# Attention in units of four heads and 128 queries instead of two heads, with 512-column value products and the compressed block filled to 128 keys

## The chip, the cores and the metric

The kernel runs on one core of one Trainium2 chip. The metric is the device time of one execution in microseconds (us). The kernel before takes 2535.07 us, the median of 3 runs (2532.68 to 2537.05).

## The reference, cut to what matters

The program is one transformer block over 1024 tokens with a width of 1024: a norm, one wide input projection, three mixers (sparse attention, RWKV-7, gated delta), gates and an output projection, then a squared-ReLU feed-forward. Only the sparse attention is touched. It has 8 heads of 64 in 2 key groups, so four heads share their keys and values. For each block of 128 queries it takes three softmaxes over the same queries: over 63 compressed keys, over the selected keys (with 16 selected blocks of 64 and 1024 tokens all causal keys are selected) and over a window of 512 keys. The three results are gated and added:

```python
s = jnp.einsum('bghqd,bgcd->bghqc', qq, kc) * scale
p_c = _masked_softmax(s, cmp_end[None, :] <= t[:, None])
o_c = jnp.einsum('bghqc,bgcd->bghqd', p_c, vc)
...
o_s = jnp.einsum('bghqk,bgqkd->bghqd', p_s, vsel)
...
o_w = jnp.einsum('bghqk,bgkd->bghqd', p_w, vwb)
o = gg[..., 0:1] * o_c + gg[..., 1:2] * o_s + gg[..., 2:3] * o_w
```

## The kernel before, in words

All products run in a split form: an operand is cast to the type fp32r (the high part) and the remainder is kept as a second tile (the low part), and products of the parts are summed in PSUM.

**Stages.** `build` (L1538) runs the norm and small columns, RWKV, the gated delta, then `nsa` (L1141), then the rest of the tail. `nsa` first prepares keys and values (`_nsa_kv`, `_nsa_compress`) and then runs `_nsa_attn` (L1267). The attention has two halves of 512 queries. `tail(0)` (L1412), the merge, output projection and feed-forward of the first 512 tokens, is put in hand as a second stream of work when the first half of the attention is written (`end_mixed`), and `tail(1)` follows when everything else is done.

**Units.** `_nsa_attn` makes 32 units. Unit u is one pair of heads `hp` by one block `qb` of 128 queries: half u // 16, pair u // 4 % 4, block u % 4 in its half. A `query` task per four units loads 512 queries of a pair, normalises them and splits them into `QH` and `QL`. `_nsa_head` (L1313) makes one head: for each of the three key sets the scores (L1339 to L1343, two products and the mask products, in one of 3 PSUM tiles "s"), the row maximum on VectorE (L1344), the exponential on ScalarE into a tile `P` (L1349), and at last the scaling of `P` by gate over sum (L1363; VectorE for the selected keys, GpSimd for the compressed and window keys). There are 4 tiles `P`, so two units have tiles at a time. `_nsa_pv` (L1366) multiplies with the values: for two blocks of 128 keys at a time, two heads each, four transposes into one PSUM tile "pt" (two of them), the cast to `PH` on ScalarE (L1391), the remainder `PL` on VectorE (L1392), then per block two products of 256 columns (`_pv_mm`, L1405) with the stationary tile V2s, V2w or V2c. The last block is the compressed one: it has 64 keys, so V2c is a stationary tile of 64 rows. `po` is then folded to `oT` (L1399 to L1402) and stored to `o_a` in HBM.

**Order of the work.** The kernel writes its instructions through a small planner, `run` (L167). A task gives back a wait in planned microseconds, or a condition, at each `yield`; the planner keeps a planned TensorE clock `te.time`. It steps the due task of lowest number. Beside it, it writes steps of the dense stream (three products of 512 columns, planned at 0.64): one for each 0.64 that attention steps have taken (`NBESIDE`, share 1.0), and one whenever no task is due. In the first half the dense stream is the remaining gate columns of the input projection (`fill`, tiles `fps<-hTh` and `fps<-hTl`), in the second it is `tail(0)`. Dense instructions get a priority number that is larger by 1000 (delta), and the first product of each step is tied behind the attention product written before it. Tile's scheduler then fixes each engine's order. Unit u may start when unit u-1 has written its heads and u-2 its value products; its value products wait for those of u-1. So the heads of one unit are planned beside the value products of the unit before.

```python
NBESIDE = (1.0, 1000, 0)
NLAT = (1.5, 3.0, 6.0, 0.3, 1.0, 3.0, 6.0, 0.6, 2.0, 0.8)
```

A head gives back 0.6 (`NLAT[7]`) after each of its three key sets, a unit 2.0 (`NLAT[8]`) between its heads and its value products, and the value products 0.8 (`NLAT[9]`) after each PSUM tile of transposes.

Of the kernel before, what the change touches and what calls it, by code (L numbers as in the profile page):

```python
# [19 lines left out]
P = 128  # L20
# [91 lines left out]
class Block:  # L112
# [1028 lines left out]
    def nsa(self):  # L1141
        tc = self.tc
        self.run(lambda: len(self.waiting) < 3 * KT and self.current is None)
        K2s, K2w = (self.tl(n, 1, [P, 2, S], F32R) for n in ("K2s", "K2w"))
        V2s, V2w = (self.tl(n, 1, [P, NST, 2, P], F32R) for n in ("V2s", "V2w"))
        K2c = self.tl("K2c", 1, [P, 2, 64], F32R)
        V2c = self.tl("V2c", 1, [64, 2, P], F32R)
        self.nsa_consts()
        self.share, self.delta, self.keep = NBESIDE
        outer = self.wk  # L1150
        with tc.tile_pool(name="nsap", bufs=1, reuse_waits="tile") as wk:
            self.wk = wk
            prep = [self.task(self._nsa_kv(br, half, K2, V2), br * 2 + half)
                    for br, (K2, V2) in enumerate(((K2s, V2s), (K2w, V2w))) for half in range(2)]
            prep.append(self.task(self._nsa_compress(K2c, V2c), 4))
            self.finish(*prep)
        with tc.tile_pool(name="nsaw", bufs=1, reuse_waits="tile") as wk:
            self.wk = wk
            self._nsa_attn(K2s, K2w, V2s, V2w, K2c, V2c)
        self.wk = outer  # L1160


    def norm64(self, x, gain, tag, out=None):
        nc = self.nc
        sq = self.tl(tag + "sq", 1)
        nc.scalar.activation(out=sq, in_=x, func=AF.Square)
        ps = self.mps("pt", 2)
        for i in range(4):
            self.te.matmul(ps[:, 2 * i:2 * i + 2], lhsT=sq[:, i * P:(i + 1) * P], rhs=self.blk64, start=True, stop=True)
        r = self.tl("r64", 2, [P, 8])  # L1170
        nc.scalar.activation(out=r, in_=ps[:, 0:8], func=AF.Sqrt, bias=self.eps)
        nc.vector.reciprocal(r, r)
        rb = self.tl(tag + "rb", 1)
        nc.gpsimd.tensor_copy(rb.rearrange("p (x d) -> p x d", d=64), r[:, :, None].to_broadcast([P, 8, 64]))
        yield NLAT[0]
        ps = self.mps("pt", 2)
# [26 lines left out]
    def _nsa_compress(self, K2c, V2c):  # L1203
        nc, a = self.nc, self.a
        tt, ts = nc.vector.tensor_tensor, nc.vector.tensor_scalar
# [3 lines left out]
        ps = self.mps("pt", 2)  # L1209
# [4 lines left out]
        ts(out=V2c, in0=self.ident[:64, None, :].to_broadcast([64, 2, P]), scalar1=0.0, scalar2=None, op0=OP.mult)  # L1214
        for x in range(2):
            kT = self.tl("kT", 1, [P, 2, S])
            src = self.nsa_in[4 + x].rearrange("(g d) s -> d g s", g=2)
# [10 lines left out]
            hp = self.mps("o", 1)  # L1228
# [9 lines left out]
            ps = self.mps("pt", 2)  # L1238
# [5 lines left out]
            ps = self.mps("pt", 2)  # L1244
# [21 lines left out]

    def _nsa_attn(self, K2s, K2w, V2s, V2w, K2c, V2c):  # L1267

        self.mark = mark = [0] * 32 + [9, 9]
        qs = {}  # L1270

        def query(i):
            half, hp = i // 4, i % 4
            nc = self.nc
            q = self.tl("q", 1)
            nc.sync.dma_start(out=q, in_=self.nsa_in[hp, :, half * 512:half * 512 + 512])
            yield NLAT[5]
            QH = self.tl("QH", 2, [P, 2, 512], F32R)
            QL = self.tl("QL", 2, [P, 2, 512], F32R)
            q = yield from self.norm64(q, self.qg, "q")  # L1280
            for e in range(2):
                h = slice(e * 64, e * 64 + 64)
                for x in (e, 1 - e):
                    nc.scalar.copy(QH[x * 64:x * 64 + 64, e], q[h])
                    nc.gpsimd.tensor_tensor(out=QL[x * 64:x * 64 + 64, e], in0=q[h], in1=QH[h, e].bitcast(F32), op=OP.subtract)
# [12 lines left out]
        self.finish(*units)  # L1298

    def _nsa_unit(self, u, qs, K, V):  # L1300
        half, hp, qb = u // 16, u // 4 % 4, u // 16 * 4 + u % 4
        g = hp // 2
        QH, QL = qs[u // 4]
# [6 lines left out]
        yield from self._nsa_pv(qb, g, hp, Ps, *V)  # L1310
        self.mark[u] = 2

    def _nsa_head(self, qb, g, H, QH, QL, K2s, K2w, K2c):  # L1313
        nc = self.nc
        tt, ts = nc.vector.tensor_tensor, nc.vector.tensor_scalar
        qs = slice(qb % 4 * P, qb % 4 * P + P)
# [18 lines left out]
        for b, pieces in enumerate(segs):  # L1335
            tiles = []
            for i, (c, keys, n, masks) in enumerate(pieces):
                ps = self.mps("s", 3)
                self.te.matmul(ps[:, :n], lhsT=QH[:, qs], rhs=keys, start=True, stop=False)  # L1339
                self.te.matmul(ps[:, :n], lhsT=QL[:, qs], rhs=keys, start=False, stop=not masks)  # L1340
# [25 lines left out]
    def _nsa_pv(self, qb, g, hp, Ps, V2s, V2w, V2c):  # L1366
        nc = self.nc
        tt = nc.vector.tensor_tensor
        k0 = max(0, qb - 4)
        blocks = [(kb * P, P, V2s[:, kb, g, :]) for kb in range(qb + 1)]  # L1370
        blocks += [(1024 + (kb - k0) * P, P, V2w[:, kb, g, :]) for kb in range(k0, qb + 1)]
        blocks += [(1664, 64, V2c[:, g, :])]
        po = self.mps("o", 1)[:, 0:256]
        last = len(blocks) - 1
        todo = []
        for b0 in range(0, len(blocks), 2):
            bl = blocks[b0:b0 + 2]
            ps = self.mps("pt", 2)
            for j, (c, n, v) in enumerate(bl):
                for e in range(2):  # L1380
                    self.te.transpose(ps[:n, (j * 2 + e) * P:(j * 2 + e + 1) * P], Ps[e][:, c:c + n], self.ident)
            PH = self.tl("PH", 3, [P, 512], F32R)
            PL = self.tl("PL", 3, [P, 512], F32R)
            runs = []
            for j, (c, n, v) in enumerate(bl):
                if runs and runs[-1][2] == n:
                    runs[-1][1] = (j + 1) * 256
                else:
                    runs.append([j * 256, (j + 1) * 256, n])
            for x0, x1, n in runs:  # L1390
                nc.scalar.copy(PH[:n, x0:x1], ps[:n, x0:x1])  # L1391
                tt(out=PL[:n, x0:x1], in0=ps[:n, x0:x1], in1=PH[:n, x0:x1].bitcast(F32), op=OP.subtract)  # L1392
            todo.append((b0, bl, PH, PL))
            if len(todo) == 2:
                self._pv_mm(po, *todo.pop(0), last)
            yield NLAT[9]
        self._pv_mm(po, *todo.pop(0), last)
        tmp = self.tl("otmp", 1, [64, 256])
        nc.scalar.copy(tmp, po[64:128])  # L1399
        oT = self.tl("oT", 2, [P, P])  # L1400
        for e in range(2):
            tt(out=oT[e * 64:e * 64 + 64], in0=po[0:64, e * P:(e + 1) * P], in1=tmp[:, e * P:(e + 1) * P], op=OP.add)  # L1402
        nc.sync.dma_start(out=self.o_spill["a"][hp, :, qb * P:(qb + 1) * P], in_=oT)

    def _pv_mm(self, po, b0, blocks, PH, PL, last):  # L1405
        for j, (c, n, v) in enumerate(blocks):
            x = slice(j * 256, (j + 1) * 256)
            self.te.matmul(po, lhsT=v, rhs=PH[:n, x], start=(b0 + j == 0), stop=False)
            self.te.matmul(po, lhsT=v, rhs=PL[:n, x], start=False, stop=(b0 + j == last))


    def tail(self, hf, wbufs):  # L1412
# [202 lines left out]
```

## Time and profile before

| | |
|---|---|
| median of 3 runs | 2535.07 us |
| profiled execution, its own time | 2527.64 us |
| its span | 2525.9 us |
| TensorE products busy | 2377.5 us (94%) |
| TensorE weight loads busy | 1907.6 us (76%) |
| VectorE / ScalarE / GpSimd busy | 1472.0 / 1043.1 / 986.8 us |
| mean granted TensorE clock | 0.965 |
| attention, first scores to last value product | 1170 to 1741 us of the span |

Engines are PE (TensorE product), PEld (its weight load), DVE (VectorE), ACT (ScalarE), POOL (GpSimd) and SP (SyncE). The duration of a product in the trace contains its way through the array, and products overlap: what one costs TensorE in a full stream is the distance from its start to the next start. A line of a timeline gives start, duration, engine, line, operation, tile written and tiles read, the rows and columns of the stationary tile (128\*128, 64\*128), the shape, and xN for N merged instructions.

### The profile page before, as it was taken

What the parts mean: (1) busy time and instruction counts of PE and PEld (TensorE: products, weight loads), DVE (VectorE), ACT (ScalarE), POOL (GpSimd) and SP (SyncE); (2) the same over time, 40 slices, a digit from 0 to 9 for tenths busy, and PEclk for the clock granted to TensorE, in tenths of its full rate; (3) what the DMA queues carried; (4) which work ended last, traced back from release to release, by engine and by line L of the source; (5) the groups of instructions that cost most, each with busy time, mean ns of one, the idle gap of its engine ahead of it and who ended that gap; (6) DMA issues with size and microseconds to landing.
All of it is one profiled execution on the core that took longest, in us unless ns stands there. A gap on an engine that the chain in (4) does not pass through costs nothing.

```text
span 2525.9 us, 37184 instructions
## 1 busy us (share of the span) xinstructions
PE 2377.5 (94%) x13589; PEld 1907.6 (76%) x13589; DVE 1472.0 (58%) x3197; ACT 1043.1 (41%) x2083; POOL 986.8 (39%) x975
## 2 busy tenths in 40 slices
PE   6979899999988999989999999999999998999999
PEld 4757676777776777777887777778888876788887
DVE  4586877663477567232556777766454436545444
ACT  5333433332344433225657665654332334423232
POOL 4444444333322121224545675344333346233232
PEclk9889889999999999989999999999999999999999
DMA  4222222222223122272213331014232354223232
GB/s 137 68 56 65 58 63 58 71 54 74 72 66 83 43 57 73 83 173 80 64 52 114 111 106 57 21 62 128 92 109 84 117 164 157 75 88 111 83 111 92
DMA packets 319718, 216.79 MB, mean 86 GB/s; under 512 B 78486, under 2 KB 273184, under 8 KB 319536
## 3 DMA queue, kind: packets, MB, share of 16 engines
q1 hardware_dynamic: 308672, 195.63, 27.3%
q10 hardware_dynamic: 9792, 17.83, 2.0%
q8 instruction: 107, 1.75, 0.3%
q0 software_dynamic: 1072, 0.96, 0.2%
q14 instruction: 75, 0.61, 0.1%
HBM read 178.16 MB, written 36.22 MB: 85 GB/s over the span
## 4 chain that ended last, share of the span: by engine, by line
PE 72%; DVE 13%; DMA 6%; ACT 4%; issue 2%; POOL 2%; SPq 0%; ACTq 0%; POOLq 0%; DVEq 0%
PE fps L97 53%; PE mps L97 15%; PE mps L101 3%; DVE inv_p L336 2%; DVE inv_u L338 1%; DVE gacc L882 1%; DVE BK L550 1%; DMA cw<-in_nsa_cmp_w_dram 1%; POOL wlo L259 1%; DMA lb<-inv 1%; ACT P L1349 1%; ACT whi L254 1%; DMA wraw<-in_w_branch_dram 1%; DVE ast L1344 1%; DMA gin<-gates 1%
## 5 line engine op out<-in xcount | busy, mean ns | idle before, releaser
L259 POOL TENSOR_TENSOR wlo<-wraw,whi 128x512 fp32r<-128x512 f32 (+2 forms) x408 | 530.0, 1302 | 878.9 <-ACT whi L254 848.5
L254 ACT CAST whi<-wraw 128x512 fp32r<-128x512 f32 (+1 forms) x408 | 286.6, 705 | 632.1 <-PE fps L97 444.8
L97 PE MATMUL fps<-hTh,whi 128*128 128x512 f32 x1024 | 447.3, 439 | 6.5 <-ACT rraw L424 3.5
L97 PE MATMUL fps<-hTh,wlo 128*128 128x512 f32 x1024 | 415.8, 410 | 1.3 <-POOL wlo L259 1.3
L97 PE MATMUL fps<-hTl,whi 128*128 128x512 f32 x1024 | 416.5, 408 | 0.0
L259 DVE TENSOR_TENSOR wlo<-wraw,whi 128x256 fp32r<-128x256 f32 (+1 forms) x207 | 129.7, 629 | 232.5 <-ACT whi L254 227.0
L97 PEld LDWEIGHTS fps<-hTh,whi 128*128 128x128 f32 x1024 | 200.9, 197 | 48.5 <-ACT rraw L424 3.6
L97 PEld LDWEIGHTS fps<-hTh,wlo 128*128 128x128 f32 x1024 | 200.0, 196 | 47.7 <-POOL wlo L259 2.2
L97 PEld LDWEIGHTS fps<-hTl,whi 128*128 128x128 f32 x1024 | 201.8, 197 | 32.3
L97 PE MATMUL fps<-h2h,whi 128*128 128x512 f32 x512 | 200.0, 391 | 1.3 <-DVE h2l L291 1.3
L1363 POOL TENSOR_SCALAR P<-P,ast 128x64 f32<-128x64 f32 (+5 forms) x128 | 137.2, 1088 | 160.0 <-DVE ast L1356 97.1
L97 PE MATMUL fps<-h2l,whi 128*128 128x512 f32 x512 | 199.6, 390 | 0.0
L97 PE MATMUL fps<-h2h,wlo 128*128 128x512 f32 x512 | 199.4, 390 | 0.0
L97 PE MATMUL fps<-whi,fl 128*128 128x512 f32 x512 | 191.0, 389 | 0.0
L97 PE MATMUL fps<-whi,fh 128*128 128x512 f32 x512 | 189.9, 391 | 0.0
L97 PE MATMUL fps<-wlo,fh 128*128 128x512 f32 x512 | 189.0, 389 | 0.0
L1442 DVE TENSOR_TENSOR acc<-fps,acc 128x512 f32<-128x512 f32 x160 | 106.7, 686 | 101.4 <-PE fps L97 101.0
L1349 ACT ACTIVATE P<-mps,ast 128x128 f32<-128x128 f32 (+4 forms) x256 | 124.9, 494 | 75.3 <-DVE ast L1347 45.5
L1344 DVE TENSOR_REDUCE ast<-mps 128x1 f32<-128x128 f32 (+4 forms) x256 | 109.0, 441 | 56.3 <-PE mps L97 53.5
L1392 DVE TENSOR_TENSOR PL<-mps,PH 128x512 fp32r<-128x512 f32 (+2 forms) x168 | 103.3, 619 | 47.7 <-ACT PH L1391 47.0
L1391 ACT CAST PH<-mps 128x512 fp32r<-128x512 f32 (+2 forms) x168 | 88.1, 533 | 63.5 <-PE mps L101 58.1
L97 PEld LDWEIGHTS fps<-h2h,whi 128*128 128x128 f32 x512 | 96.2, 188 | 21.5 <-DVE h2l L291 1.8
(465 smaller groups left out, 4802.0 us busy)
## 6 DMA issues: line engine op xcount, KB each, us to landing
wraw<-in_w_in_dram SPq DMA_DIRECT2D x152, 256.0 KB, 2.9
wraw<-in_w_ff_dram SPq DMA_DIRECT2D x128, 256.0 KB, 2.8
wraw<-in_w_ff_dram SPq DMA_DIRECT2D x64, 512.0 KB, 3.4
gates<-fst ACTq DMA_DIRECT2D x48, 256.0 KB, 2.0
wraw<-in_w_branch_dram SPq DMA_DIRECT2D x48, 256.0 KB, 3.2
gin<-gates SPq DMA_DIRECT2D x48, 256.0 KB, 3.2
wraw<-in_w_out_dram SPq DMA_DIRECT2D x16, 512.0 KB, 3.5
nsa_in<-fst ACTq DMA_DIRECT2D x20, 256.0 KB, 2.1
```

The costliest lines, as they stand in the source:

```text
L97: return self.note(self.nc.tensor.matmul(out, lhsT=lhsT, rhs=rhs, **kw))
L101: return self.note(self.nc.tensor.transpose(out, x, ident))
L254: nc.scalar.copy(hi, raw)
L259: eng.tensor_tensor(out=lo[:, x], in0=raw[:, x], in1=hi[:, x].bitcast(F32), op=OP.subtract)
L336: nc.vector.tensor_tensor(out=v, in0=lt[:n, s, None, s + 1:].to_broadcast([n, w, w]), in1=u[:n, s + 1:, s + 1:].rearrange("p t c -> p c t" ...
L338: nc.vector.tensor_reduce(out=u[:n, s, s + 1:], in_=v, axis=AX, op=OP.add)
L1344: nc.vector.tensor_reduce(out=(mx if i == 0 else mx2)[:, b:b + 1], in_=ps[:, :n], axis=AX, op=OP.max, negate=True)
L1349: nc.scalar.activation(out=Pt[:, c:c + n], in_=tiles[i][:, :n], func=AF.Exp, bias=mx[:, b:b + 1], accum_out=(sm if i == 0 else sm2)[:, b:b ...
L1363: eng.tensor_scalar(out=Pt[:, c:c + n], in0=Pt[:, c:c + n], scalar1=r[:, b:b + 1], scalar2=None, op0=OP.mult)
L1391: nc.scalar.copy(PH[:n, x0:x1], ps[:n, x0:x1])
L1392: tt(out=PL[:n, x0:x1], in0=ps[:n, x0:x1], in1=PH[:n, x0:x1].bitcast(F32), op=OP.subtract)
L1442: tt(out=acc[:, st, c0:c0 + 512], in0=ps, in1=acc[:, st, c0:c0 + 512], op=OP.add)
```

## The change

A unit is now a key group of four heads by 128 queries, so there are 16. Its query task covers four heads and 256 queries. All four tiles `P` belong to one unit, and a unit may start only when the unit before has written its value products (`mark[u - 1] >= 2`); the wait between `mark` of the heads and the value products is gone. In the value products each PSUM tile holds one block of 128 keys for four heads, and each product has 512 columns; there are two per block, one PSUM tile behind the transposes. The tile `P` grows from 1728 to 1792 columns, GpSimd writes zeros to the last 64 at the start of each head, and V2c gets 128 rows, the last 64 of them zero, so the compressed block is a block like the others. The output tile holds four heads and is stored by one DMA. The tile `qrb` of the query norm shares the buffer of `qsq`.

```diff
-        V2c = self.tl("V2c", 1, [64, 2, P], F32R)
+        V2c = self.tl("V2c", 1, [P, 2, P], F32R)
...
-        rb = self.tl(tag + "rb", 1)
+        rb = self.tl("qsq" if tag == "q" else tag + "rb", 1, name=tag + "rb")
...
+            half, g, j = i // 4, i // 2 % 2, i % 2
+            q = self.tl("q", 1, [P, 2, 256])
+            QH = self.tl("QH", 2, [P, 2, 2, 256], F32R)
+            QL = self.tl("QL", 2, [P, 2, 2, 256], F32R)
...
-        for u in range(32):
-            if u % 4 == 0:
-                i = u // 4
-                self.task(query(i), u - 5, lambda i=i: i == 0 or ((i - 1) in qs and mark[4 * i - 5] >= 2))
+        for u in range(16):
+            if u % 2 == 0:
+                i = u // 2
+                self.task(query(i), u - 2, lambda i=i: i == 0 or ((i - 1) in qs and mark[2 * i - 3] >= 1))
...
-                                   lambda u=u: u // 4 in qs and mark[u - 1] >= 1 and mark[u - 2] >= 2))
-        self.run(lambda: mark[15] >= 2)
+                                   lambda u=u: u // 2 in qs and mark[u - 1] >= 2))
+        self.run(lambda: mark[7] >= 2)
...
-        for e in range(2):
-            Ps.append((yield from self._nsa_head(qb, g, 2 * hp + e, QH[:, e], QL[:, e], *K)))
+        for h in range(4):
+            lhs = (Q[:, h // 2, h % 2, t] for Q in (QH, QL))
+            Ps.append((yield from self._nsa_head(qb, g, 4 * g + h, *lhs, *K)))
         self.mark[u] = 1
-        yield lambda: self.mark[u - 1] >= 2
         yield NLAT[8]
...
-        Pt = self.tl("P", 4, [P, 1728])
+        Pt = self.tl("P", 4, [P, 1792])
+        nc.gpsimd.memset(Pt[:, 1728:1792], 0.0)
...
+        def product():
+            i, v, PH, PL = todo.popleft()
+            self.te.matmul(po, lhsT=v, rhs=PH, start=(i == 0), stop=False)
+            self.te.matmul(po, lhsT=v, rhs=PL, start=False, stop=(i == last))
+
+        for i, (c, v) in enumerate(blocks):
             ps = self.mps("pt", 2)
+            for h in range(4):
+                self.te.transpose(ps[:, h * P:(h + 1) * P], Ps[h][:, c:c + P], self.ident)
...
+            nc.scalar.copy(PH, ps)
+            tt(out=PL, in0=ps, in1=PH.bitcast(F32), op=OP.subtract)
+            todo.append((i, v, PH, PL))
             if len(todo) == 2:
+                product()
             yield NLAT[9]
+        product()
+        tmp = self.tl("otmp", 1, [64, 512])
...
+        oT = self.tl("oT", 1, [P, 2, P])
```

## Rows read from the trace of the kernel before

**Rows 1.** The page, part 1: TensorE's products.

```profile
PE 2377.5 (94%) x13589; PEld 1907.6 (76%) x13589; DVE 1472.0 (58%) x3197; ACT 1043.1 (41%) x2083; POOL 986.8 (39%) x975
```

**Rows 2.** Busy time by stretch: from:to, length, each engine (instructions), granted clock, DMA.

```profile
1157.00:1346.80 189.80, 187.82 (x1090) 154.20 (x1089) 94.97 (x264) 119.34 (x315) 96.04 (x100) 0.99 0.20 60
1346.80:1371.40 24.60, 22.16 (x138) 17.08 (x136) 19.88 (x54) 18.00 (x55) 15.76 (x15) 0.93 0.54 177
1371.40:1610.00 238.60, 229.70 (x1326) 187.50 (x1326) 184.56 (x404) 154.16 (x389) 152.71 (x114) 0.99 0.27 84
```

**Rows 3.** Timeline of TensorE around one unit's two products with V2c.

```profile
1204.48 0.60 PE L101 MATMUL mps<-ident,P 128*128 128x128 f32 x4
1204.83 0.48 PE L97 MATMUL fps<-hTh,whi 128*128 128x512 f32 x1
1205.15 0.39 PE L97 MATMUL fps<-hTl,whi 128*128 128x512 f32 x1
1205.38 0.40 PE L97 MATMUL fps<-hTh,wlo 128*128 128x512 f32 x1
1205.71 0.38 PE L97 MATMUL mps<-PH,V2c 64*128 64x256 f32 x1
1206.02 0.49 PE L97 MATMUL fps<-hTh,whi 128*128 128x512 f32 x1
1206.44 0.38 PE L97 MATMUL mps<-PL,V2c 64*128 64x256 f32 x1
1206.75 0.44 PE L101 MATMUL mps<-ident,P 128*128 128x128 f32 x2
```

**Rows 4.** Timeline of TensorE around the last two products with V2c.

```profile
1740.71 0.38 PE L97 MATMUL mps<-PH,V2c 64*128 64x256 f32 x1
1740.93 0.28 PE L97 MATMUL mps<-PL,V2c 64*128 64x256 f32 x1
1741.14 0.50 PE L97 MATMUL fps<-h2h,whi 128*128 128x512 f32 x1
```

**Rows 5.** Timeline of TensorE: a dense product, full value products, transposes of 64 columns.

```profile
1211.99 0.39 PE L97 MATMUL fps<-hTh,wlo 128*128 128x512 f32 x1
1212.22 0.28 PE L97 MATMUL mps<-PL,V2s 128*128 128x256 f32 x1
1212.33 0.28 PE L97 MATMUL mps<-PH,V2w 128*128 128x256 f32 x1
1212.45 0.28 PE L97 MATMUL mps<-PL,V2w 128*128 128x256 f32 x1
1212.57 0.38 PE L101 MATMUL mps<-ident,P 128*64 128x128 f32 x2
1212.71 0.48 PE L97 MATMUL fps<-hTh,whi 128*128 128x512 f32 x1
```

**Rows 6.** Groups by shape, whole attention: count, busy us, mean ns, idle before.

```profile
L97 PE MATMUL mps<-PH,V2c 64*128 64x256 f32 x32 | 12.2, 383 | 1.2 <-ACT PH L1391 1.2
L1392 DVE TENSOR_TENSOR PL<-mps,PH 128x512 fp32r<-128x512 f32 x128 | 87.2, 684 | 31.3 <-ACT PH L1391 30.7
```

**Rows 7.** Groups by shape, whole run, GpSimd: zeros of 128x64 elsewhere in the kernel.

```profile
L388 POOL MEMSET gmask<- 128x64 f32 x2 | 0.2, 151 | 0.0
```

**Rows 8.** Groups by shape on TensorE, 1157 to 1346.8: one of three fill products.

```profile
L97 PE MATMUL fps<-hTl,whi 128*128 128x512 f32 x145 | 58.5, 406 | 0.0
```

**Rows 9.** Timeline of TensorE: the last fill product and the first of the tail.

```profile
1346.61 0.39 PE L97 MATMUL fps<-hTh,wlo 128*128 128x512 f32 x1
...
1371.38 0.48 PE L97 MATMUL fps<-oh,whi 128*128 128x512 f32 x1
```

**Rows 10.** Groups by shape on TensorE, 1346.8 to 1371.4.

```profile
L101 PE MATMUL mps<-ident,P 128*128 128x128 f32 x29 | 5.6, 306 | 0.0
...
L97 PE MATMUL mps<-K2c,QL 128*128 128x64 f32 x5 | 1.4, 277 | 0.0
```

**Rows 11.** Busy time by stretch: one in which no dense product ran.

```profile
1620.00:1640.00 20.00, 16.24 (x90) 13.88 (x90) 14.76 (x40) 18.19 (x41) 4.49 (x4) 0.74 0.06 17
```

More of the change, by code (lines that the diff above doesn't have):

```diff
@@ L1213, in _nsa_compress @@
         nc.vector.tensor_copy(pos2[64:128], pv[:, :, 16:32])
-        ts(out=V2c, in0=self.ident[:64, None, :].to_broadcast([64, 2, P]), scalar1=0.0, scalar2=None, op0=OP.mult)
+        ts(out=V2c, in0=self.ident[:, None, :].to_broadcast([P, 2, P]), scalar1=0.0, scalar2=None, op0=OP.mult)
         for x in range(2):
@@ L1267, in _nsa_attn @@
     def _nsa_attn(self, K2s, K2w, V2s, V2w, K2c, V2c):
-        self.mark = mark = [0] * 32 + [9, 9]
+        self.mark = mark = [0] * 16 + [9, 9]
         qs = {}
         def query(i):
-            half, hp = i // 4, i % 4
+            half, g, j = i // 4, i // 2 % 2, i % 2
             nc = self.nc
-            q = self.tl("q", 1)
-            nc.sync.dma_start(out=q, in_=self.nsa_in[hp, :, half * 512:half * 512 + 512])
+            q = self.tl("q", 1, [P, 2, 256])
+            t0 = half * 512 + j * 256
+            nc.sync.dma_start(out=q, in_=self.nsa_in[2 * g:2 * g + 2, :, t0:t0 + 256].rearrange("x p t -> p x t"))
             yield NLAT[5]
-            QH = self.tl("QH", 2, [P, 2, 512], F32R)
-            QL = self.tl("QL", 2, [P, 2, 512], F32R)
-            q = yield from self.norm64(q, self.qg, "q")
+            QH = self.tl("QH", 2, [P, 2, 2, 256], F32R)
+            QL = self.tl("QL", 2, [P, 2, 2, 256], F32R)
+            yield from self.norm64(q.rearrange("p x t -> p (x t)"), self.qg, "q")
             for e in range(2):
@@ L1283, in query @@
                 for x in (e, 1 - e):
-                    nc.scalar.copy(QH[x * 64:x * 64 + 64, e], q[h])
-                    nc.gpsimd.tensor_tensor(out=QL[x * 64:x * 64 + 64, e], in0=q[h], in1=QH[h, e].bitcast(F32), op=OP.subtract)
+                    o = slice(x * 64, x * 64 + 64)
+                    nc.scalar.copy(QH[o, :, e], q[h])
+                    nc.gpsimd.tensor_tensor(out=QL[o, :, e], in0=q[h], in1=QH[h, :, e].bitcast(F32), op=OP.subtract)
             yield NLAT[6]
@@ L1300, in _nsa_unit @@
     def _nsa_unit(self, u, qs, K, V):
-        half, hp, qb = u // 16, u // 4 % 4, u // 16 * 4 + u % 4
-        g = hp // 2
-        QH, QL = qs[u // 4]
+        g, qb = u // 4 % 2, u // 8 * 4 + u % 4
+        t = slice(u % 2 * P, u % 2 * P + P)
+        QH, QL = qs[u // 2]
         Ps = []
-        for e in range(2):
-            Ps.append((yield from self._nsa_head(qb, g, 2 * hp + e, QH[:, e], QL[:, e], *K)))
+        for h in range(4):
+            lhs = (Q[:, h // 2, h % 2, t] for Q in (QH, QL))
+            Ps.append((yield from self._nsa_head(qb, g, 4 * g + h, *lhs, *K)))
         self.mark[u] = 1
-        yield lambda: self.mark[u - 1] >= 2
         yield NLAT[8]
-        yield from self._nsa_pv(qb, g, hp, Ps, *V)
+        yield from self._nsa_pv(qb, g, Ps, *V)
         self.mark[u] = 2
@@ L1338, in _nsa_head @@
                 ps = self.mps("s", 3)
-                self.te.matmul(ps[:, :n], lhsT=QH[:, qs], rhs=keys, start=True, stop=False)
-                self.te.matmul(ps[:, :n], lhsT=QL[:, qs], rhs=keys, start=False, stop=not masks)
+                self.te.matmul(ps[:, :n], lhsT=QH, rhs=keys, start=True, stop=False)
+                self.te.matmul(ps[:, :n], lhsT=QL, rhs=keys, start=False, stop=not masks)
                 for j, (mo, m) in enumerate(masks):
@@ L1364, in _nsa_head, with _nsa_pv @@
         return Pt
-    def _nsa_pv(self, qb, g, hp, Ps, V2s, V2w, V2c):
+    def _nsa_pv(self, qb, g, Ps, V2s, V2w, V2c):
         nc = self.nc
@@ L1369, in _nsa_pv @@
         k0 = max(0, qb - 4)
[L1370 to L1373, printed above, removed]
+        blocks = [(kb * P, V2s[:, kb, g, :]) for kb in range(qb + 1)]
+        blocks += [(1024 + (kb - k0) * P, V2w[:, kb, g, :]) for kb in range(k0, qb + 1)]
+        blocks += [(1664, V2c[:, g, :])]
+        po = self.mps("o", 1)
@@ L1374, in _nsa_pv @@
         last = len(blocks) - 1
-        todo = []
-        for b0 in range(0, len(blocks), 2):
-            bl = blocks[b0:b0 + 2]
+        todo = deque()
+        def product():
[3 more added lines that the diff above has]
+        for i, (c, v) in enumerate(blocks):
             ps = self.mps("pt", 2)
-            for j, (c, n, v) in enumerate(bl):
-                for e in range(2):
-                    self.te.transpose(ps[:n, (j * 2 + e) * P:(j * 2 + e + 1) * P], Ps[e][:, c:c + n], self.ident)
+            for h in range(4):
+                self.te.transpose(ps[:, h * P:(h + 1) * P], Ps[h][:, c:c + P], self.ident)
@@ L1382, in _nsa_pv @@
             PH = self.tl("PH", 3, [P, 512], F32R)
             PL = self.tl("PL", 3, [P, 512], F32R)
[L1384 to L1392, printed above, removed]
@@ L1393, in _nsa_pv @@
-            todo.append((b0, bl, PH, PL))
+            nc.scalar.copy(PH, ps)
+            tt(out=PL, in0=ps, in1=PH.bitcast(F32), op=OP.subtract)
+            todo.append((i, v, PH, PL))
             if len(todo) == 2:
-                self._pv_mm(po, *todo.pop(0), last)
+                product()
             yield NLAT[9]
-        self._pv_mm(po, *todo.pop(0), last)
-        tmp = self.tl("otmp", 1, [64, 256])
+        product()
+        tmp = self.tl("otmp", 1, [64, 512])
         nc.scalar.copy(tmp, po[64:128])
-        oT = self.tl("oT", 2, [P, P])
+        oT = self.tl("oT", 1, [P, 2, P])
@@ L1401, in _nsa_pv @@
+        h4 = lambda ap: ap.rearrange("p (x e t) -> p x e t", x=2, e=2)
         for e in range(2):
[L1402 to L1409, printed above, removed]
+            tt(out=oT[e * 64:e * 64 + 64], in0=h4(po[0:64])[:, :, e], in1=h4(tmp)[:, :, e], op=OP.add)
@@ L1412, in tail @@
+        nc.sync.dma_start(out=self.o_spill["a"][2 * g:2 * g + 2, :, qb * P:(qb + 1) * P].rearrange("x p t -> p x t"), in_=oT)
     def tail(self, hf, wbufs):
```

1 line of the change is left out of this document (removed).

## The prediction
> **What bounds the kernel now.** I read the page's shares first: TensorE is busy for 94% of the span and no other engine for more than 58% [rows 1]. Then the table by stretch: while the first half of the attention runs beside the fill (1157 to 1346.8), TensorE is busy for 187.82 of 189.80 us and VectorE for half of it; later, beside the tail, 229.70 of 238.60 [rows 2]. So where dense products are at hand, the attention costs what it puts on TensorE and its waits cost almost nothing. The exception is the stretch between: the last fill product starts at 1346.61, the first product of the tail at 1371.38, and in these 25 us the attention is alone [rows 9]. There VectorE has 19.88 and ScalarE 18.00 of 24.60 [rows 2]: a chain in which TensorE waits. Two questions follow: how much TensorE work goes, and whether the stretch without dense work grows.
>
> Third view: TensorE's timeline, where I take distances between starts. In a full stream a 512-column product takes 0.23 and a 256-column value product 0.11 to 0.12 [rows 5]: in proportion to the columns. Four transposes take 0.35, and the product behind them 0.32 in place of 0.23: 0.09 for the turn [rows 3]. A product with V2c (64 rows) takes 0.31 (1205.71 to 1206.02, 1206.44 to 1206.75), and the full product before it is also longer, 0.33 in place of 0.23 [rows 3]. No idle mark stands there.
>
> **The change part by part.**
>
> *Columns.* There are 74 key blocks over the eight query blocks (36 selected, 30 window, 8 compressed). Before: 74 x 4 pairs x 2 = 592 products of 256 columns, at 0.117 69.3 us if all were full. After: 74 x 2 groups x 2 = 296 products of 512, at 0.23 68.1. Gain 1.2. Half as many weight loads bring nothing more, since the distance already goes with the columns.
>
> *The 64 rows.* The 64 products with V2c (32 with PH [rows 6], as many with PL) each cost 0.31 - 0.12 = 0.19 of their own and 0.10 in the product before: 0.29, and 64 x 0.29 = 18.6 is the upper bound. Where the two stand together, as the last two do, they take 0.22 and 0.21 [rows 4], 0.10 each too much: 64 x 0.10 = 6.4 is the lower bound. I take 17, near the upper end, since the separated pair is what a unit plans (PH and PL become ready one after the other, with other work between). With 128 rows I expect nothing of it to be left.
>
> *Transposes.* Still 592; the PSUM tiles of four go from 160 to 148 (74 x 2), 12 turns of 0.09 less: 1.1. The 64 transposes of 64 columns take 0.07 each (two in 0.14) [rows 5] and become full ones of 0.09 [rows 3]: 1.3 more. Together nothing. By the Trainium skill (TensorEngine Tiling (Array Packing), Key Properties) any change of the array's mode drains TensorE, and its list of modes has 64 columns beside 64 rows; by that rule the 32 pairs of such transposes would drain too and, at 0.29 each, give back 9 us more. The trace shows no drain there: the product before takes its 0.12 and the pair 0.14 [rows 5], so I leave the 9 out.
>
> *Other engines.* VectorE and ScalarE handle the same columns in 148 pieces of 512 in place of 128 of 512, 8 of 256 and 32 of 64x256; VectorE at 0.684 [rows 6] gains a few us, not on the path while TensorE is full [rows 2]. GpSimd gets 64 clears of 128x64, at 0.151 [rows 7] 9.7 us; it has 96.04 of 189.80 [rows 2], so they cost nothing by themselves. But each is the first instruction of a head in GpSimd's queue and waits until the old tile P has been transposed; behind it stand the scalings of P and the weight remainders for the dense stream (L259). If the scheduler puts it early, those weights come late and dense products wait. The queries have the same elements in eight tasks; the load in pieces of 1 KB has a planned 3 us and comes up to two units ahead. The qsq/qrb buffer costs nothing: the copy needs r, which needs the products that read qsq.
>
> *The order.* This takes something back. Before, the heads of one unit ran beside the value products of the unit before. Now all four tiles P belong to one unit and it waits for the last one's value products; on each engine the exponentials of the next unit are queued behind that. Each yield thus finds no other attention task, and the planner writes dense steps into it. Walking the planner's loop by hand: a head gives at least 3 steps, a value block 2, the 2.0 wait 3. The first four units (16 heads, 24 blocks) take 48 + 48 + 12 = 108, and up to 130 with the shares owed. The trace has about 145 steps in all from the first query on (one of their three products is counted x145 [rows 8]). Before they lasted into unit 13 of 16 of this half; now they last into the fifth or sixth of eight.
>
> The rest runs as the stretch 1346.8 to 1371.4 does now. It held 29 full transposes and a few short ones, some 35, or 8.75 of the new blocks, and five heads [rows 10]. Left are 8 heads and 16 blocks to 12 heads and 21 blocks (query blocks 1 to 3), 1.7 to 2.4 times that: 42 to 59 us at its rate. TensorE's need, an estimate: a block 0.35 + 0.09 + 2 x 0.23 = 0.90, a head's scores (four products of 0.17 to 0.23, two small ones, masks and turns) 1.3, a query 2: 14.4 + 10.4 + 2 = 27 to 18.9 + 15.6 + 4 = 38. Idle 15 to 21, where the stretch of now has, by the same prices and six V2c products, 24.6 - (7.9 + 6.5 + 1.7 + 1) = 7.5. So 7 to 14 more. Bounds: 0 if the priority number (1000 higher for dense) keeps dense steps for the end, 27 if the two phases in series add some 4.5 us in each of three units. I take 9.
>
> *The border of the halves.* The tail's first branch reads o_a of the first half. Before, three of its four tiles were complete early and only the last pair's was late; now the last unit completes two. The tail's first two PSUM tiles can then run 12 products before they wait, in place of 18: 6 x 0.23 = 1.4 less cover, bounds 0 and 5 (the attention may be at hand, or not). I take 1.4.
>
> *Second half.* Dense work is plentiful: all of `tail(0)`. Idle in 1371.4 to 1610 is 8.9 [rows 2]; with more dense steps per attention step it may fall, with the new chain it may rise: 0, bounds 9 either way.
>
> **Sum.** -1.2 - 17 + 9 + 1.4 = -7.8 us. The profiled execution took 2527.64 (span 2525.9), so it would take 2519.8; it stands 7.4 below the median of the runs, 2535.07, so the median becomes 2527.3.
>
> **Rivals.**
> 1. *Nothing is given back* (chance 0.20). The dense steps' later priority holds them until TensorE would idle; the fill then outlasts the attention. For it: 187.82 of 189.80 busy [rows 2] leaves no idle time that would have used the fill up early. Against: the fill did end before the attention. -18.2, and up to 6 less idle: 2511 to 2517.
> 2. *Starved and slow clock* (0.22). In the last three units of the first half TensorE waits so much that its clock drops to the lower of its two levels, 1.2 GHz. In 1620 to 1640, with no dense product, the granted clock was 0.74 [rows 11], in 1346.8 to 1371.4 0.93 [rows 2]. Price: 27 for the chain in series (18 over my 9), and 38 us of TensorE work at 0.74 take 13 more, about half on the chain: 6. -7.8 + 24 = +16: 2551. It decides from where TensorE's idle time in the first half grows by more than 17. A page of the Trainium skill (TensorE: Matmul & The Clock Gate, Part 1) also has a waiting TensorE fall to the slower clock; the trace agrees at 0.74.
> 3. *The 64 rows are not the cause* (0.10): the V2c products are slow because they are last, waiting for their PH and PL, and the filled ones stay so. Only the 6.4 goes: -1.2 - 6.4 + 10.4 = +2.8, 2538. Against: the product before is longer as well, and without an idle mark [rows 3].
>
> **How the numbers follow.** My forecast (0.48) covers 2519 to 2536 and its middle is 2527. About 0.2% (5 us) is what a measurement can tell from no change, so faster is below 2530: 0.33 of the forecast and rival 1's 0.20, 0.53. Same takes 0.15 of the forecast and 0.07 of rival 3, 0.22. Slower: rival 2 and the rest of rival 3, 0.25. The range reaches into rival 1 and to just short of rival 2's middle: 2510 to 2549.
>
> **What would show it.** Products with V2c read 128\*128 and start 0.23 apart; value products count 296; the last fill product starts before the sixth unit's value products, and from there to the first tail product lie 40 to 60 us with TensorE idle for 15 to 21; the clock stays at 0.99 elsewhere. I am wrong if V2c products stay over 0.3, if the fill lasts to within 25 us of the tail, or if idle time grows beside the tail.

## The result and the profile after

The changed kernel takes 2611.02 us, the median of 4 runs (2608.31 to 2618.41), against 2533.88 for the kernel before (4 runs, 2532.05 to 2537.05): a ratio of 1.0308 with a 95% interval of 1.0283 to 1.0333. It is 77 us slower, and the forecast of 2527 with its range of 2510 to 2549 is wrong. The profiled execution took 2612.75 (span 2611.0), 85.1 above that of before, and its mean granted clock is 0.945 in place of 0.965. Line numbers behind the changed part have moved: the row maximum is L1347, the exponential L1352, the clear of a tile `P` L1320, the cast to `PH` L1392.

The page, part 1 (busy us, share, instructions), beside [rows 1]:

```profile
PE 2411.1 (92%) x13293; PEld 1912.5 (73%) x13293; DVE 1442.7 (55%) x3126; ACT 1049.0 (40%) x2049; POOL 1005.0 (38%) x1039
```

TensorE has 296 products fewer and stands more. Where it stands is seen in the last fill product and the first of the tail (timeline, beside [rows 9]), and in busy time by stretch, cut at these two and at the last value product (beside [rows 2]: from:to, length, each engine with its instructions, granted clock, DMA):

```profile
1317.06 0.48 PE L97 MATMUL fps<-hTh,wlo 128*128 128x512 f32 x1
...
1408.23 0.63 PE L97 MATMUL fps<-oh,whi 128*128 128x512 f32 x2
```

```profile
1162.80:1317.10 154.30, 149.19 (x811) 122.68 (x809) 58.50 (x158) 85.09 (x208) 74.41 (x89) 1.00 0.23 68
1317.10:1408.20 91.10, 72.08 (x311) 51.84 (x310) 47.03 (x127) 51.80 (x136) 43.13 (x59) 0.70 0.17 55
1408.20:1888.50 480.30, 429.81 (x2094) 337.36 (x2093) 288.93 (x603) 257.32 (x595) 238.26 (x194) 0.93 0.22 69
```

The stretch without dense work is 91 us long, not 25, at a granted clock of 0.70. Beside the tail the attention is slower as well: 480 us, in which TensorE is busy for 89%. In the trace of before the same part, 1371.4 to 1741, took 369.6 with TensorE busy for 352.98 (96%). The tail executed 999 dense products of 512 columns there in place of 729. At 0.23 each these 270 are 62 of the 111 us more, work that would have come later; the rest is loss.

To compare kernels I count *stalls*: for each line of TensorE's timeline (a product, or a few merged ones), what the distance from its start to the next start has beyond the distance in a full stream at the full clock, where that excess is over 0.25 us. The sums move by up to 4 us with the distances that one takes for a full stream, so smaller differences between them are not read. "First half" runs up to the tail's first product, "second half" from there to the last value product. Before: 7.6 and 27.3. After: 48.6 and 73.5. So 41.0 and 46.2 more, 87.2 together. The excess of the V2c products and of the products before them falls from 16.8 to 1.8, the turns behind transposes cost 4.9 less, delays of under 0.25 each 13.2 more, and the attention's need at those distances rises by 0.8: 87.2 - 15.0 - 4.9 + 13.2 + 0.8 = 81.3 of the 85.1; the other 4 lie outside the attention (it starts 4.6 later in this trace).

What TensorE waited for (view of waits, 1163 to 1888: engine, line, cause; us in total, times, longest), of the kernel after and then of the kernel before (1158 to 1741):

```profile
PEld mps L97 <- ACT P L1352: 61.9, 53, 5.1
...
PE mps L97 <- ACT P L1352: 48.7, 41, 4.9
POOL P L1320 <- PE mps L101: 35.0, 11, 8.8
```

```profile
PEld mps L97 <- ACT P L1349: 13.9, 21, 1.9
...
PE mps L97 <- ACT P L1349: 7.0, 11, 1.7
```

A product of scores waits for an exponential, which has to free one of the three PSUM tiles "s". This wait has grown from 7.0 to 48.7 us, most of it beside the tail (the same view from 1408 to 1888, then that of before from 1371 to 1741):

```profile
PE mps L97 <- ACT P L1352: 36.3, 29, 4.9
```

```profile
PE mps L97 <- ACT P L1349: 4.7, 8, 1.3
```

Two places show how it arises. First, the stretch without dense work (timeline; the bracket is the idle time before and what ended it):

```profile
1325.60 1.06 PE L101 MATMUL mps<-ident,P 128*128 128x128 f32 x4
...
1326.06 0.31 ACT L1352 ACTIVATE P<-mps,ast 128x64 f32<-128x64 f32 x1 [1.34 <-PE mps L101]
1326.15 0.73 POOL L1320 MEMSET P<- 128x64 f32 x4 [2.72 <-PE mps L101]
...
1329.32 0.62 ACT L254 CAST whi<-wraw 128x512 fp32r<-128x512 f32 x1 [1.47 <-DMA wraw<-in_w_branch_dram]
1329.85 0.31 ACT L1352 ACTIVATE P<-mps,ast 128x64 f32<-128x64 f32 x1
...
1330.30 0.30 PE L97 MATMUL mps<-K2c,QH 128*128 128x64 f32 x1 [1.17 <-ACT P L1352]
...
1332.73 1.28 ACT L1171 ACT_TABLE_LOAD   x1
...
1334.31 1.28 ACT L1352 ACT_TABLE_LOAD   x1
...
1336.22 0.58 PE L97 MATMUL mps<-K2s,QH 128*128 128x256 f32 x1 [1.19 <-ACT P L1352]
```

The first exponential and the four clears of the next unit stand until the transposes of the unit before have read the tiles `P`; then TensorE stands for the exponentials. The tiles are not the whole of these two waits. Ahead of the exponential at 1329.85 ScalarE had stood 1.47 us for a weight of the tail (cast L254), and ahead of the one before 1336.22 it loaded its tables twice, 1.28 us each, for the root in the query norm (L1171) and back for the exponential. The kernel before loads its tables for the root as often (eight times at L1171 in either trace), and its TensorE waited for exponentials for only 7.0 us in all. Second, beside the tail, where dense work is at hand:

```profile
1532.74 0.39 PE L101 MATMUL mps<-ident,P 128*128 128x128 f32 x2
...
1534.69 1.34 DVE L1473 SCALAR_TENSOR_TENSOR ms<-ms,mh 128x512 fp32r<-128x512 f32 x1
...
1536.56 0.61 DVE L1350 TENSOR_TENSOR ast<-ast 128x1 f32<-128x1 f32 x1
...
1537.20 0.69 ACT L1352 ACTIVATE P<-mps,ast 128x512 f32<-128x512 f32 x1 [2.46 <-DVE ast L1350]
...
1538.03 0.47 PE L97 MATMUL mps<-K2w,QH 128*128 128x128 f32 x1 [4.90 <-ACT P L1352]
...
1538.61 0.78 PE L97 MATMUL fps<-oh,whi 128*128 128x512 f32 x1
```

TensorE stands for 4.90 us with a score product at the front of its queue. The exponential it needs waits for the smaller of two negated row maxima (L1350), which on VectorE stood behind a piece of the tail's merge (L1473) and another row maximum. The dense product `fps<-oh` stands behind the score product and does not get past it. At 1538.61 that product and the next start 0.58 apart: from 1538.0 to 1539.7 the granted clock is 0.50.

Two counts from the same traces show what has changed in the order. Of the exponentials of a unit, before, 156 of 160 in the second half started ahead of the last value product of the unit before; after, it is 30 of 160 (the first half is in the table below). And from one score product with QH to the next, no value product and no transpose stood in between in 64 of 148 cases before and in 113 of 152 after (from the tail's first product on).

What the change was to remove is gone. The products with V2c on TensorE's timeline, beside [rows 3], and the groups by shape, beside [rows 6] (count, busy us, mean ns, idle before):

```profile
1209.26 0.39 PE L97 MATMUL fps<-hTl,whi 128*128 128x512 f32 x1
1209.48 0.40 PE L97 MATMUL mps<-PL,V2c 128*128 128x512 f32 x1
1209.72 0.28 PE L97 MATMUL mps<-blk,qsq 128*128 128x2 f32 x2
```

```profile
L1393 DVE TENSOR_TENSOR PL<-mps,PH 128x512 fp32r<-128x512 f32 x148 | 100.6, 688 | 114.3 <-ACT PH L1392 114.1
...
L1320 POOL MEMSET P<- 128x64 f32 x64 | 7.6, 152 | 38.0 <-PE mps L101 35.0 <-PE mps L97 2.6 <-POOL P L1320 0.2
L97 PE MATMUL mps<-PH,V2c 128*128 128x512 f32 x16 | 7.6, 477 | 0.0
```

A V2c product now takes 0.24 for 512 columns, and the product before it 0.22. Most V2c products with PH now stand right behind transposes and take about 0.32; that is the turn that a dense product of 512 columns has there too [rows 3].

### The profile page after: what moved, and what is told of

Its sections match the earlier page's. It is cut to its first block, busy times and chain, and to the rows that moved or that the text cites. A ratio compares the mean times of both kernels' runs of the same rounds, so it can differ in the third digit from the quotient of the medians.

```text
span 2611.0 us, 36491 instructions
## 1 busy us (share of the span) xinstructions
PE 2411.1 (92%) x13293; PEld 1912.5 (73%) x13293; DVE 1442.7 (55%) x3126; ACT 1049.0 (40%) x2049; POOL 1005.0 (38%) x1039
## 5 line engine op out<-in xcount | busy, mean ns | idle before, releaser
L259 POOL TENSOR_TENSOR wlo<-wraw,whi 128x512 fp32r<-128x512 f32 (+2 forms) x408 | 539.9, 1325 | 926.1 <-ACT whi L254 881.5
L254 ACT CAST whi<-wraw 128x512 fp32r<-128x512 f32 (+1 forms) x408 | 286.9, 705 | 612.0 <-PE fps L97 420.3
L97 PEld LDWEIGHTS fps<-hTh,whi 128*128 128x128 f32 x1024 | 201.5, 197 | 48.7 <-ACT rraw L424 3.7
L259 DVE TENSOR_TENSOR wlo<-wraw,whi 128x256 fp32r<-128x256 f32 (+1 forms) x188 | 113.6, 608 | 210.2 <-ACT whi L254 205.1
L1352 ACT ACTIVATE P<-mps,ast 128x128 f32<-128x128 f32 (+4 forms) x256 | 124.4, 492 | 103.3 <-DVE ast L1350 58.5
L1393 DVE TENSOR_TENSOR PL<-mps,PH 128x512 fp32r<-128x512 f32 x148 | 100.6, 688 | 114.3 <-ACT PH L1392 114.1
L1347 DVE TENSOR_REDUCE ast<-mps 128x1 f32<-128x128 f32 (+4 forms) x256 | 110.2, 444 | 87.5 <-PE mps L97 83.2
L1392 ACT CAST PH<-mps 128x512 fp32r<-128x512 f32 x148 | 84.8, 587 | 118.1 <-PE mps L101 116.9
L101 PE MATMUL mps<-ident,P 128*128 128x128 f32 x592 | 105.2, 292 | 11.7 <-DVE P L1366 10.1
```

The lines of the kernel that those rows point to most:

```text
L97: return self.note(self.nc.tensor.matmul(out, lhsT=lhsT, rhs=rhs, **kw))
L101: return self.note(self.nc.tensor.transpose(out, x, ident))
L254: nc.scalar.copy(hi, raw)
L259: eng.tensor_tensor(out=lo[:, x], in0=raw[:, x], in1=hi[:, x].bitcast(F32), op=OP.subtract)
L1347: nc.vector.tensor_reduce(out=(mx if i == 0 else mx2)[:, b:b + 1], in_=ps[:, :n], axis=AX, op=OP.max, negate=True)
L1352: nc.scalar.activation(out=Pt[:, c:c + n], in_=tiles[i][:, :n], func=AF.Exp, bias=mx[:, b:b + 1], accum_out=(sm if i == 0 else sm2)[:, b:b ...
```

## The experiments

The theory (A): with all four tiles `P` in one unit, a unit's softmax and its value products run in series, tile by tile; TensorE's queue keeps its order, so dense work behind a waiting product does not help. Rivals: (B) the fill is used up too early because of the planned waits; (C) the clears on GpSimd hold the tiles; (D) the planned order alone, units in series, costs the time. e1 ran four times, the other variants once; in the four runs of the changed kernel the times lie within 10 us, so differences of up to 10 us between single runs are not read. The kernel before took 2532.82 (median of 7), 2533.68 and 2531.09 in the three sessions of these runs.

**e1: the fill alone.** The kernel before, with its units of two heads; only the compressed block is filled, the clears included.

```diff
-        V2c = self.tl("V2c", 1, [64, 2, P], F32R)
+        V2c = self.tl("V2c", 1, [P, 2, P], F32R)
...
-        Pt = self.tl("P", 4, [P, 1728])
+        Pt = self.tl("P", 4, [P, 1792])
+        nc.gpsimd.memset(Pt[:, 1728:1792], 0.0)
...
-        blocks += [(1664, 64, V2c[:, g, :])]
+        blocks += [(1664, P, V2c[:, g, :])]
```

> The kernel before with the compressed block filled to 128 keys (V2c of 128 rows, P of 1792 columns, GpSimd's clears, the shared qsq buffer) and nothing else. If the 64 rows cost what the prediction said (17 us) and the clears on GpSimd cost nothing: 2514 to 2520 us. If the 64 rows are not the cause: 2527 to 2535. If the clears in GpSimd's queue are what made the changed kernel slow: above 2545.

Measured: 2517.05 us (4 runs, 2512.37 to 2521.75), ratio to before 0.9929 (0.9902 to 0.9957): 15.8 faster. TensorE's timeline, and the clears among the groups by shape:

```profile
1197.37 0.40 PE L97 MATMUL fps<-hTh,wlo 128*128 128x512 f32 x1
1197.61 0.28 PE L97 MATMUL mps<-PL,V2c 128*128 128x256 f32 x1
1197.73 0.27 PE L101 MATMUL mps<-ident,P 128*128 128x128 f32 x1
```

```profile
L1318 POOL MEMSET P<- 128x64 f32 x64 | 8.0, 152 | 19.1 <-PE mps L101 16.4 <-PE mps L97 2.6
```

The product takes 0.12 and the one before it 0.24. The excess around V2c is 2.0 us in place of 16.8. All 64 clears are in this kernel, so by themselves they are not the loss (against C); e3 below has none and loses as much. This is the version that beats both kernels.

**e2: the order in series, four tiles.** The kernel before; a unit of two heads starts only when the unit before has written its value products. Four tiles `P` are still two units' worth.

```diff
-                                   lambda u=u: u // 4 in qs and mark[u - 1] >= 1 and mark[u - 2] >= 2))
+                                   lambda u=u: u // 4 in qs and mark[u - 1] >= 2))
```

> The kernel before (two heads, four tiles P), but a unit may be written only when the unit before has written its value products, as in the changed kernel. Theory A, that the four tiles P of one unit keep the next unit's exponentials out of the value products: this kernel still has two units' tiles, so the time stays within 15 us of before (2520 to 2550). Theory B, that the planner puts a dense step into every wait and uses the fill up early: the stretch between the last fill product and the tail's first grows from 25 to over 60 us, and the time to over 2570.

Measured: 2527.57, 5 below the median of before: no loss. The stretch without dense work (first line) did grow to 54 us, at a clock of 0.84:

```profile
1322.60:1376.70 54.10, 48.37 (x287) 38.20 (x285) 37.51 (x109) 38.64 (x109) 29.67 (x31) 0.84 0.26 85
1376.70:1795.50 418.80, 404.29 (x2260) 334.19 (x2259) 300.19 (x618) 249.21 (x603) 237.50 (x167) 0.98 0.25 77
```

Theory B had asked for over 60 us and over 2570. So neither the planned order (D) nor a longer stretch without dense work costs this much by itself: with tiles at hand, the next unit's exponentials run beside this unit's value products whatever the order planned (90 of 90 and 156 of 160 start ahead of its last value product, as before).

**e3: the same with two tiles.** One unit's worth, as in the changed kernel.

```diff
-        Pt = self.tl("P", 4, [P, 1728])
+        Pt = self.tl("P", 2, [P, 1728])
```

> As the run before it, but with two tiles P in place of four, so that all tiles belong to one unit as in the changed kernel; products stay at 256 columns and 64 rows. Theory A: most of the loss appears only here, 2600 us or more (before plus the 77 of the changed kernel and the 17 that the 64 rows keep), and TensorE idles beside the tail too. Theory B: no more than 15 us over the run before it.

Measured: 2611.61, 84 above e2 for this one number. Stretches and waits (as above, 1158 to 1918):

```profile
1304.50:1414.70 110.20, 88.79 (x423) 67.87 (x422) 58.75 (x159) 59.79 (x166) 44.92 (x49) 0.72 0.16 51
1414.70:1918.00 503.30, 460.27 (x2441) 374.28 (x2440) 311.87 (x647) 269.63 (x635) 253.83 (x178) 0.96 0.23 71
```

```profile
PEld mps L97 <- ACT P L1349: 41.8, 43, 3.5
...
PE mps L97 <- ACT P L1349: 30.9, 26, 3.2
```

The picture of the changed kernel, in a kernel that has none of its other parts: 110 us without dense work at 0.72, and the wait for the exponential at 30.9 us. Of the exponentials 55 of 90 and 52 of 160 still start ahead of the last value product of the unit before. That is theory A.

**e10: three tiles**, between the two (e2 with `self.tl("P", 3, ...)`).

> Two heads in series with three tiles P, between the runs with four (2527.6) and two (2611.6). Theory A: between the two, 2545 to 2590, since one head of the next unit can run beside the value products. If any tile too few stops the overlap: 2600 to 2612.

Measured: 2547.45. With 4, 3 and 2 tiles: 2527.6, 2547.5, 2611.6. The first tile missing costs 20, the second 64.

**e6: two tiles, in series, with the fill** (e1 with the edits of e2 and e3).

> Two heads in series with two tiles P as in the third run, and the compressed block filled as in the first. If TensorE's work still sets the time there, the 16 us of the first run come back: 2593 to 2598. If the chain sets it and TensorE only waits longer: 2604 to 2612, and then the changed kernel at 2611 has lost its 16 us in the same way.

Measured: 2598.02, 13.6 below e3. The gain of the fill comes off the loss, as far as single runs tell. The changed kernel, the median of its four runs, is another 13 us slower. What it has beyond e6 (four heads per unit, products of 512 columns, queries in eight tasks, one output tile) is not taken apart here.

**e4: the planned waits away**, so that the planner has no such waits to fill with dense steps.

```diff
-NLAT = (1.5, 3.0, 6.0, 0.3, 1.0, 3.0, 6.0, 0.6, 2.0, 0.8)
+NLAT = (1.5, 3.0, 6.0, 0.3, 1.0, 3.0, 6.0, 0.0, 2.0, 0.0)
```

> The changed kernel with the planned waits after a key set and after a value block set from 0.6 and 0.8 to 0, so that the planner writes fewer dense steps per attention step and the fill lasts through the first half. Theory B: the stretch without dense products shrinks from 91 us to under 40 and the time falls to 2560 to 2575. Theory A: the same idle time appears beside the dense products instead; the time stays within 20 us of 2611.

Measured: 2600.64, 10 below the median of the changed kernel and 8 below its fastest run. Stretches (fill, none, tail):

```profile
1154.10:1365.90 211.80, 197.33 (x1088) 156.62 (x1087) 106.94 (x275) 126.96 (x328) 108.38 (x140) 0.98 0.18 55
1365.90:1379.50 13.60, 10.36 (x47) 7.37 (x46) 7.33 (x23) 9.66 (x26) 4.03 (x4) 0.67 0.77 251
1379.50:1804.00 424.50, 361.89 (x1784) 280.81 (x1784) 263.37 (x565) 228.68 (x546) 207.71 (x179) 0.93 0.20 61
```

The fill now lasts almost to the tail, and 68 us are still lost against before. First-half stalls fell by 20.5, those beside the tail rose by 15.0. The stretch shrank as theory B said, to 13.6 us, and the time did not follow. So the early end of the fill (B) is where much of the loss shows, not what makes most of it.

**e5: fixed tiles.** The changed kernel; the four tiles are allocated once for the whole attention and the zeros are written once.

```diff
+        self.Pt = [self.tl("P%d" % h, 1, [P, 1792]) for h in range(4)]
+        for t in self.Pt:
+            self.nc.gpsimd.memset(t[:, 1728:1792], 0.0)
...
-        Pt = self.tl("P", 4, [P, 1792])
-        nc.gpsimd.memset(Pt[:, 1728:1792], 0.0)
+        Pt = self.Pt[H % 4]
```

> The changed kernel with the four tiles P made once and kept, so that a part of a tile may be written again as soon as that part is transposed, not when the whole tile is; the zeros are written once, so the 64 clears are gone too. Theory A (the tiles P hold the next unit back): part of the loss comes back, 2560 to 2595. If the clears in GpSimd's queue or the four heads in series cost the time, whatever is free in P: clears 2600 to 2606 (7.6 us of clears and some of their waits), series 2605 to 2615.

Measured: 2596.61, 14.4 below: just above theory A's range, and below those of both rivals. A part of a tile can be written again once that part has been transposed, and no clear waits; the run doesn't separate the two. Stalls: 43.7 and 63.9. Most of the loss stays; a unit's heads still need all four tiles.

**e8: e5 with the value blocks in the order in which a head writes its parts** (compressed, selected, window).

> As the run with kept tiles, and the value blocks taken in the order compressed, selected, window, in which the next unit's exponentials need the parts. Theory A: 10 us or more below that run, since the part that is needed first is free first; 2540 to 2580. If the order of freeing does not matter: within 6 us of it.

Measured: 2591.46. 5 below e5, where theory A had 10 or more: within what single runs can differ by, so unclear.

**e7: six tiles in the first half.** There a tile needs only 1152 columns, so six fit. The second half keeps four of 1792. The edit is cut to the tiles; the columns of the parts move with them.

```diff
...
-        Pt = self.tl("P", 4, [P, 1792])
-        nc.gpsimd.memset(Pt[:, 1728:1792], 0.0)
+        wb, cb = (512, 1024) if qb < 4 else (1024, 1664)
+        Pt = self.pp.tile([P, cb + P], F32, name="P", tag="P", bufs=6 if qb < 4 else 4)
+        nc.gpsimd.memset(Pt[:, cb + 64:cb + P], 0.0)
...
```

> The changed kernel with P laid out in 1152 columns in the first half (512 selected, 512 window, 128 compressed) and six tiles of it there in the same memory; four tiles of 1792 in the second half as before. Theory A: idle time of TensorE in the first half falls by half or more (48 us of stalls to 25 or less), the time to 2580 to 2595; the second half keeps its stalls. If the tiles are not it: 2605 to 2615.

Measured: 2592.58, 18.4 below the changed kernel. First-half stalls 30.1 in place of 48.6 (the expectation had 25 or less), second half 75.6, about unchanged.

**e9: eight tiles in the first half**, two units' worth, and there the conditions of before as well (a unit may start when the unit before has written its heads; a query task waits until a unit's value products are written, not only its heads). The edit is against e7.

```diff
-                self.task(query(i), u - 2, lambda i=i: i == 0 or ((i - 1) in qs and mark[2 * i - 3] >= 1))
+                self.task(query(i), u - 2, lambda i=i: i == 0 or ((i - 1) in qs and mark[2 * i - 3] >= 2))
...
-                                   lambda u=u: u // 2 in qs and mark[u - 1] >= 2))
+                                   lambda u=u: u // 2 in qs and mark[u - 1] >= (1 if u < 8 else 2) and mark[u - 2] >= 2))
...
+        yield lambda: self.mark[u - 1] >= 2
         yield NLAT[8]
...
-        Pt = self.pp.tile([P, cb + P], F32, name="P", tag="P", bufs=6 if qb < 4 else 4)
+        Pt = self.pp.tile([P, cb + P], F32, name="P", tag="P", bufs=8 if qb < 4 else 4)
```

> The changed kernel with eight tiles P of 1152 columns in the first half, and there the planned order of the kernel before (a unit's heads beside the value products of the unit before); the second half as in the changed kernel. Theory A: the first half's stalls fall from 49 us (30 with six tiles) to 15 or less, and the time to 2565 to 2580, the rest of the loss staying in the second half. If four heads in series cost by themselves, with tiles at hand: the first half keeps 25 us or more, and the time stays at 2585 to 2595.

Measured: 2569.39, 41.6 below the changed kernel. Stretches (without dense work, beside the tail):

```profile
1340.50:1359.60 19.10, 15.80 (x95) 11.74 (x93) 10.75 (x24) 13.10 (x29) 6.60 (x10) 1.00 0.70 228
1359.60:1844.00 484.40, 433.99 (x2097) 340.24 (x2098) 301.43 (x606) 256.37 (x599) 246.88 (x201) 0.93 0.22 68
```

The first half is whole again: 19 us without dense work, clock 1.00. The second line is that of the changed kernel almost to the number. The loss that is left sits in the half that still has four tiles. No run gives the second half of the changed kernel more tiles.

The last two columns count the exponentials of a unit that start ahead of the last value product of the unit before, in the first and the second half.

| kernel | us | stalls, first half | stalls, second half | early exponentials, first half | second half |
|---|---|---|---|---|---|
| before (profiled execution) | 2527.64 | 7.6 | 27.3 | 90 of 90 | 156 of 160 |
| after (profiled execution) | 2612.75 | 48.6 | 73.5 | 35 of 84 | 30 of 160 |
| e1 fill alone (time: median of 4) | 2517.05 | 6.5 | 35.1 | 90 of 90 | 154 of 160 |
| e2 in series, 4 tiles | 2527.57 | 15.6 | 21.2 | 90 of 90 | 156 of 160 |
| e10 in series, 3 tiles | 2547.45 | 24.7 | 27.7 | 90 of 90 | 127 of 160 |
| e3 in series, 2 tiles | 2611.61 | 47.1 | 58.4 | 55 of 90 | 52 of 160 |
| e6 e3 with fill | 2598.02 | 47.9 | 59.6 | 54 of 90 | 48 of 160 |
| e4 no planned waits | 2600.64 | 28.1 | 88.5 | 33 of 84 | 28 of 160 |
| e5 fixed tiles | 2596.61 | 43.7 | 63.9 | 41 of 84 | 51 of 160 |
| e8 e5, parts in order | 2591.46 | 37.6 | 59.6 | 64 of 84 | 64 of 160 |
| e7 six tiles, first half | 2592.58 | 30.1 | 75.6 | 70 of 84 | 28 of 160 |
| e9 eight tiles, first half | 2569.39 | 9.5 | 74.0 | 79 of 84 | 26 of 160 |

## Why the prediction was wrong, point by point

*Columns, transposes, other engines: right to a few us.* The attention's need on TensorE changed by 0.8 us where the sum had -1.2, and the turns behind transposes cost 4.9 us less where it had 1.1; the 9 us for a drain at the 64-column transposes were rightly left out. The rule of the Trainium skill (TensorEngine Tiling (Array Packing), Key Properties) that a change of mode drains the array agrees with what the 64-row products cost here; at the 64-column transposes no trace here shows a drain (the pair takes 0.14 and the product before it 0.12 [rows 5]). The clears take 7.6 us on GpSimd. The way in which they could hurt, behind the transposes of the old tile, is to be seen (35.0 us of GpSimd waiting), but e1 has them without a loss.

*The 64 rows: right.* I took 17 of 6.4 to 18.6. e1 measures 15.8, and the distances give 15.0 between the kernels. Rival 3 (they are slow because they are last) is out: in e1 they are still last and take 0.12.

*The order: wrong, and the step that failed.* The fill did end in the fifth unit, as worked out, at 1317. But then I wrote "The rest runs as the stretch 1346.8 to 1371.4 does now" and priced it at that rate: 42 to 59 us, +9, bounds 0 to 27. That stretch held two units side by side, with four tiles for two units. I had seen that all four tiles now belong to one unit, and had the chain in series as a bound only, 4.5 us in each of three units. It took 91 us. Part of that is more work than reckoned: 23 blocks and 15 heads (three of them of the next half) in place of 16 to 21 and 8 to 12, which at the rate of before would be 65 to 74 us. The rest is the rate. By the prediction's own prices TensorE's need there is 23 x 0.90 + 15 x 1.3 + 4 = 44, so 47 of the 91 us were idle or slow, 39 more than the 7.5 of before, where the sum had 7 to 14. The first half's stalls grew by 41.0; six tiles give 18.5 of that back (e7), and eight with the order that they allow 39.1 (e9). The planned order, which I took for the cause, costs nothing with four tiles (e2).

*Second half: wrong.* I took 0, bounds 9, because "dense work is plentiful". It is, and TensorE stands beside it: 46.2 us more. The wait for the exponential is 31.6 of that (4.7 to 36.3). A plentiful stream helps only if a product of it is next in the queue, as the 4.90 us at 1538.03 show. Before, value products or transposes stood between the scores of two key sets in 84 of 148 cases and gave the softmax time; now they do in 39 of 152, and with three PSUM tiles "s" a score product waits for the exponential of the third tile before it. That missing tiles do this beside the tail too is shown for units of two heads (second-half stalls 21.2, 27.7, 58.4 with 4, 3, 2 tiles). For the changed kernel it is argued, from the same wait and from 30 early exponentials of 160 where there were 156; the tail's own work on VectorE and ScalarE, which stands in front of some of the exponentials, may have a share in it.

*The border: small, as said.* From 1408 to 1888 TensorE waits only 1.2 us for the tail's first operand (`oh`).

*Rival 2 (starved, slow clock)* was the right mechanism in the right place, the first half: it charged 33 for the order, and 41.0 was measured, with the clock at 0.70 where it took 0.74. It ended at 2551 since it, too, left the second half at 0; with the 46.2 it would have been 2597. Rival 1 (the fill outlasts the attention) is out: the fill ended 91 us before the tail.

## What to carry to other kernels

Count the buffers in units of work, not in tiles: a change that doubles the unit and leaves the number of tiles halves the depth, and a wait of TensorE that took 7.0 us in the profile of before takes 48.7. The rate of a stretch may be carried over only if what ran side by side there still can. Test the parts of a change alone: the fill by itself is worth 16 us, and the rest of the change costs about 94 (e1 to the changed kernel).

## What was unexpected about the hardware

A stationary tile of 64 rows among tiles of 128 cost 0.23 us per product here (15.0 us for 64 in the distances), part of it in the product before; that is as much as 512 columns of a full tile, and zeros in the other 64 rows removed it (e1: 0.12 per product). A stationary tile of 64 columns (the transposes of rows 5) cost nothing of the kind.

The granted clock was 0.70 on the mean of a stretch of 91 us, so TensorE ran at both its levels, 1.2 and 2.4 GHz, and more at the lower. It was busy there for 72.08 us, and no single wait in that stretch is longer than 1.85 us: it stood 23 times for more than 0.2 us, 18.3 us in all. In e9 the stretch without dense work, 19 us long with TensorE busy for 15.80, ran at 1.00.
